# First layer's shift and scale: 128x128 weight blocks held and two columns moved, and six load buffers

## The chip, the cores and the metric

The kernel runs on one core of a Trainium2 chip. The core has a matrix engine (PE in the profile; its weight loads are listed apart as PEld), a vector engine (DVE), a scalar engine (ACT), a general engine (POOL), and a queue that issues transfers (SP). The metric is the device time of one execution in microseconds (us), lower being better. Three timed executions of the kernel before gave 2374.71, 2380.99 and 2374.34 us, so its median is 2374.71 us.

## The reference, cut to what matters

A two-layer backbone takes latent tokens x (1024 x 1024), context tokens ctx (256 x 1024) and two conditioning vectors. Each layer first turns the conditioning vectors into shifts, scales and gates, and the normalized tokens are modulated with them before any projection can run:

```
mod_lat = (silu_c @ mod_w[l] + mod_b[l])        # latent tokens
mod_ctx = silu_cc @ mod_w[l] + mod_b[l]         # context tokens
sh1, sc1, g1, sh2, sc2, g2 = split(mod_lat, 6)  # 1024 values each
h_lat = rms_norm(x, norm1_g[l]) * (1 + sc1) + sh1
h_ctx = rms_norm(ctx, norm1_g[l]) * (1 + csc1) + csh1
out   = mix(h_lat @ w_in, h_ctx @ w_in)         # retention and attention heads
```

Only sh1 and sc1 of the first layer matter here, each for both conditioning vectors: two vectors of 1024 times a 1024 x 2048 slice of `mod_w[0]`. The other ten parts are made later in another way.

## The kernel before, in words

Tokens lie transposed: a tile holds 128 channels (partitions) by up to 1024 tokens, so x is eight tiles `x_t[k]` and ctx one tile `ctx_t` of eight slices. A shift or a scale is therefore wanted as a column of 128 partitions per slice k: `sh1` and `gs1` (scale times gain), filled by `mod_cols`.

The start of the program does the following. SP issues the loads in the order in which the code names them, with at most eight in flight, and a load into a ring tile waits until the tile's last reader is done. ACT squares ctx and x, DVE adds the squares up (`start_sum`), PE sums over partitions (`norm_rstd`, tile nsum, a 128x128 block held and one column moved), POOL takes the power -0.5 (tile rs), and PE spreads the result over partitions (`norm_bc`, tile nbc). Beside that `mod_row(part, k)` loads a 128 x 1024 piece of `mod_w` (tile mw, a ring of three) and multiplies: the two conditioning columns `scc[:, k, :]` are held, 512 columns are moved, and the result is two rows of 1024 (tile modrow). Part 1 is the scale, part 0 the shift, eight pieces each. When a part's eight pieces are in, ACT copies the rows to SBUF (tile rsb), PE transposes them in eight steps into columns (tile mcol), and DVE adds the bias.

With the scale there, DVE multiplies all tokens by scale and norm (L266); with the shift there, ACT and DVE make the split operands h and hc (L276, L277), and the first projection begins: tiles pc (context) and pl (latent), by `mm3` (L75 to L77), three matmuls a product. Its weights (tile st, `in_wg`) are loaded and split by ACT (L80) and POOL (L81) beside the rest. All later work of the kernel follows from this projection.

A float32 matmul of the program stands in the trace as two passes, each with its own weight load. The instructions of one engine run in the order in which the tile framework leaves them, which for these lines is nearly that of the code.

Of the kernel before, what the change touches and what calls it, by code (L numbers as in the profile page):

```python
# [10 lines left out]
F32 = mybir.dt.float32  # L11
# [5 lines left out]
P = 128  # L17
D = 1024
KT = D // P
T = 1024  # L20
NTT = T // P
TC = 256
H = 512
# [3 lines left out]
NHID = 32  # L27
NW = 12
NPRO = 8
WCOL = 2 * H  # L30


def hybrid_retention_gqa_chunkmlp_kernel(tc, I, out):
    nc = tc.nc
    PSUM = bass.MemoryType.PSUM

    def open_pool(name, bufs=1, **kw):
        st = ExitStack()
        pool = st.enter_context(tc.tile_pool(name=name, bufs=bufs, **kw))
        return pool, st.close  # L40

    const, close_const = open_pool("const")
    stage, close_stage = open_pool("stage")
    sring = [stage.tile([P, WCOL], F32, name=f"st{i}") for i in range(3)]
    snext = [0]
    wpool, close_w = open_pool("wpool")
    wring = [wpool.tile([P, WCOL], F32R, name=f"wr{i}") for i in range(NW)]
    wnext = [0]
# [5 lines left out]
    def mm_tile(shape, name):  # L54
        if banks:
            return banks[0].tile(shape, F32, tag="b", bufs=8, name=name)
        return psum.tile(shape, F32, tag="mm", bufs=2, name=name)

    def aux_tile(shape, name):
        if banks:  # L60
            return banks[0].tile(shape, F32, tag="b", bufs=8, name=name)
        return psum.tile(shape, F32, tag="aux", bufs=4, name=name)
# [20 lines left out]
    def load_w(src, name, eng=nc.vector):  # L83
        st = st_tile()
        nc.sync.dma_start(st, src)
        hi, lo = w_tile(), w_tile()
        split(st, hi, lo, eng)
        return hi, lo


    ident = const.tile([P, P], F32, name="ident")
# [11 lines left out]
    scc = const.tile([P, KT, 2], F32, name="scc")  # L103
    nc.scalar.activation(scc, cc, AF.Silu)

    start, close_start = open_pool("start", side="right")
    startx, close_startx = open_pool("startx", side="right")
    ctx_t = start.tile([P, KT, TC], F32, name="ctx_t")
    x_t = [startx.tile([P, T], F32, tag="x0", bufs=8, name=f"x0_{k}") for k in range(KT)]
# [3 lines left out]
    gs1 = const.tile([P, 2, KT], F32, name="gs1")  # L113

    def mod_cols(part, dst):
        rsb = start.tile([2, D], F32, tag="rsb", bufs=1, name=f"rsb{part}")
        nc.scalar.copy(rsb, rows[part])
        mcol = aux_tile([P, 8, 2], f"mcol{part}")
        for j in range(8):
            nc.tensor.transpose(mcol[:, j, :], rsb[:, j * P:(j + 1) * P], ident[:2, :2])  # L120
        for s in range(2):
            nc.vector.tensor_tensor(dst[:, s, :], mcol[:, :, s], modb[:, 0, part * 8:part * 8 + 8], ALU.add)
            if part == 1:
                nc.vector.scalar_tensor_tensor(dst[:, s, :], dst[:, s, :], 1.0, gains[:, 0, :], ALU.add, ALU.mult)
# [66 lines left out]
    def norm_rstd(pool, ss, w):  # L191
        n = w // P
        pc = aux_tile([P, 8], "nsum")
        for t in range(n):
            nc.tensor.matmul(pc[:, t:t + 1], lhsT=ss[:, t * P:(t + 1) * P], rhs=ones, start=True, stop=True)
        ms = pool.tile([P, 8], F32, tag="ms", bufs=2, name="ms")
        nc.vector.tensor_scalar(ms[:, :n], pc[:, :n], 1.0 / D, EPS, ALU.mult, ALU.add)
        rs = pool.tile([P, 8], F32, tag="rs", bufs=2, name="rs")
        nc.gpsimd.tensor_tensor(rs[:, :n], ms[:, :n], mhalf[:, :n], ALU.pow)
        return rs  # L200

    def norm_bc(rs, w):
        pb = aux_tile([P, w], "nbc")
        for t in range(w // P):
            nc.tensor.matmul(pb[:, t * P:(t + 1) * P], lhsT=rs[:, t:t + 1].broadcast_to([P, P]), rhs=ident,
                             start=True, stop=True)
        return pb
# [4 lines left out]
    parts = [([ctx_t[:, k, :] for k in range(KT)], TC, 1,  # L212
              [(hc[k // 2][:, k % 2, 0, :], hc[k // 2][:, k % 2, 1, :]) for k in range(KT)])]
# [3 lines left out]
    def p_weight(gi, j):  # L217
        return load_w(I["wg"][gi, 2 * j:2 * j + 2].rearrange("k p n -> p k n"), f"g{gi}_{j}",
                      nc.vector if gi else nc.gpsimd)

    def start_sum(srcs, w, i):
        ss = start.tile([P, T], F32, tag="ssx", bufs=1, name=f"ssx{i}")[:, :w]
        for k in range(KT):
            sq = start.tile([P, T], F32, tag="sqx", bufs=2, name="sqx")[:, :w]
            nc.scalar.activation(sq, srcs[k], AF.Square)
            if k == 1:
                nc.vector.tensor_tensor(ss, sq0, sq, ALU.add)
            elif k > 1:
                nc.vector.tensor_tensor(ss, ss, sq, ALU.add)
            sq0 = sq  # L230
        return ss

    rows = [mm_tile([2, D], f"modrow{part}") for part in range(2)]

    def mod_row(part, k):
        st = start.tile([P, WCOL], F32, tag="mw", bufs=3, name=f"mw0_{k}_{part}")
        nc.sync.dma_start(st, I["mod_w"][0, k * P:(k + 1) * P, part * D:(part + 1) * D])
        for j in range(2):
            nc.tensor.matmul(rows[part][:, j * H:(j + 1) * H], lhsT=scc[:, k, :],
                             rhs=st[:, j * H:(j + 1) * H], start=(k == 0), stop=(k == KT - 1))  # L240

    W0 = []
    for i in range(4):
        mod_row(1, i)
        for k in (2 * i, 2 * i + 1):
            nc.sync.dma_start(x_t[k], I["xT"][k * P:(k + 1) * P, :])
    pbs = [norm_bc(norm_rstd(start, start_sum(parts[0][0], TC, 0), TC), TC)]
    for k in range(4, KT):
        mod_row(1, k)
        if k == 5:  # L250
            W0.append(p_weight(0, 0))
    ss_x = start_sum(x_t, T, 1)
    for k in range(KT):
        if k == 1:
            mod_cols(1, gs1)
        if k == 2:
            rs_x = norm_rstd(start, ss_x, T)
        if k == 3:
            for hf in range(2):
                pbs.append(norm_bc(rs_x[:, 4 * hf:4 * hf + 4], H))  # L260
        mod_row(0, k)
        if k in (0, 3, 5):
            W0.append(p_weight(0, len(W0)))
    for (srcs, w, s, _), pb in zip(parts, pbs):
        for k in range(KT):
            nc.vector.scalar_tensor_tensor(srcs[k], srcs[k], gs1[:, s, k:k + 1], pb, ALU.mult, ALU.mult)  # L266
    mod_cols(0, sh1)
    for i, (srcs, w, s, outs) in enumerate(parts):
        cw = w if i == 2 else TC
# [59 lines left out]
    for h in range(NH):  # L329
        for d in range(2):  # L330
            j = d * NH + h
# [235 lines left out]
    nt, close_nt = open_pool("nt")  # L567
    sring.append(nt.tile([P, WCOL], F32, name="st3"))
    yf_pool, close_yf = open_pool("yf")
# [273 lines left out]
    def up_first(l, F, s_d, e_d):  # L843

        for p0 in range(0, NPRO, 2):
            ps = [mm_tile([P, H], f"uf{l}_{p0 + d}") for d in range(2)]
# [81 lines left out]
    def layer_mlp(l, F, close_xt, s_d, e_d, x1_d, done):  # L928
# [5 lines left out]
        turns = iter(range(10000))  # L934
        mlp_up(l, F, s_d, lambda n: ring[next(turns) % 16], {p: e_d[p] for p in range(NPRO)})
        close_up()
# [7 lines left out]
    def scratch(l):  # L944
        s_d = [dram.tile([7, P, H], F32, name=f"s_d{l}_{p}") for p in range(16)]
        e_d = [dram.tile([P, H], F32, name=f"e_d{l}_{p}") for p in range(NPRO)]
        x1_d = dram.tile([KT, P, T], F32, name=f"x1_d{l}")
# [216 lines left out]
```

## Time and profile before

| what | value |
|---|---|
| timed executions, median | 2374.71 us |
| profiled execution, own time | 2382.32 us |
| its span, first to last instruction | 2380.5 us |
| PE busy | 2254.3 us, 95% of the span |
| DVE, ACT, POOL busy | 69%, 43%, 6% |
| chain that ended last, by engine | PE 78%, DVE 9%, DMA 6%, ACT 3% |
| mean granted clock of PE | 0.976 |

The page gives one execution's busy times, the chain of work that ended last followed back from the end, and the costliest groups of instructions. Times in the rows are microseconds from the start of the span; a mean duration is in nanoseconds. PE's clock has two levels in these rows, 2.4 GHz (1.00) and 1.2 GHz (0.50). A matmul's own duration contains the way through the array; what a stream of them costs is read from the starts, so from a row's duration divided by its count.

### The profile page before, as it was taken

The numbers are of one execution on the slowest core, as the hardware profiler recorded it, in microseconds if no ns is written. First come the engines' busy times: TensorE is split into PE (matmuls) and PEld (weight loads), VectorE is DVE, ScalarE is ACT, GpSimd is POOL, SyncE is SP. The second block draws the span as 40 slices with busy tenths as digits, with TensorE's granted clock in tenths as the row PEclk, the third lists the DMA queues.
The fourth block names the chain that finished last, engine by engine and source line by source line (L and its number), as shares of the span: only waits on it lengthen the run. The fifth ranks groups of instructions, "written<-read, shape, count | busy, mean of one in ns | idle before, by whom it ended". The sixth has DMA issues, their size and how long they took to land.

```text
span 2380.5 us, 28904 instructions
## 1 busy us (share of the span) xinstructions
PE 2254.3 (95%) x10412; PEld 1810.1 (76%) x10412; DVE 1651.0 (69%) x2750; ACT 1028.3 (43%) x1837; POOL 144.1 (6%) x133
## 2 busy tenths in 40 slices
PE   6998999989999999989999959999999999799999
PEld 1887787778887778867778847888878888677777
DVE  5656678699857776558888663444678755798885
ACT  3511112288745545554444333222465555544441
POOL 2322221100000000000000010000000000000000
PEclk9998999989999999999999979999999999899999
DMA  8244556430154664465454341114447444845442
GB/s 292 72 137 146 157 185 187 154 124 25 48 186 127 232 209 153 137 236 179 149 148 146 92 137 51 47 45 168 137 141 244 168 146 135 285 153 148 144 136 83
DMA packets 158688, 350.72 MB, mean 147 GB/s; under 512 B 16592, under 2 KB 30416, under 8 KB 158544
## 3 DMA queue, kind: packets, MB, share of 16 engines
q1 hardware_dynamic: 154960, 336.28, 43.6%
q0 software_dynamic: 3584, 12.58, 1.4%
q8 instruction: 82, 1.34, 0.2%
q14 instruction: 62, 0.51, 0.1%
HBM read 262.29 MB, written 86.51 MB: 147 GB/s over the span
## 4 chain that ended last, share of the span: by engine, by line
PE 78%; DVE 9%; DMA 6%; ACT 3%; issue 2%; POOL 1%; SPq 0%; DVEq 0%; ACTq 0%; POOLq 0%
PE dbd L75 5%; PE ub L75 4%; PE dbd L77 4%; PE dbd L76 4%; PE ub L76 4%; PE ub L77 4%; PE po L76 3%; PE po L77 3%; PE po L75 2%; PE ue L75 2%; PE ue L77 2%; PE ue L76 2%; PE ded L75 2%; PE ded L76 2%; PE ded L77 2%; PE pl L77 2%
## 5 line engine op out<-in xcount | busy, mean ns | idle before, releaser
L80 ACT CAST wr<-st 128x512 fp32r<-128x512 f32 (+4 forms) x422 | 281.0, 672 | 509.3 <-PE dbd L76 84.2
L81 DVE TENSOR_TENSOR wr<-st,wr 128x512 fp32r<-128x512 f32 (+4 forms) x418 | 310.3, 748 | 183.7 <-ACT wr L80 142.6
L75 PE MATMUL dbd<-sT,wr 128*128 128x512 f32 x384 | 157.1, 409 | 30.3 <-DVE xd L890 23.5
L75 PE MATMUL ub<-T,wr 128*128 128x512 f32 x384 | 153.1, 399 | 7.1 <-ACT wr L80 4.8
L75 PE MATMUL pl<-wr,h 128*128 128x512 f32 x384 | 154.8, 403 | 0.3 <-ACT zrl L484 0.3
L76 PE MATMUL dbd<-sT,wr 128*128 128x512 f32 x384 | 154.3, 402 | 0.0
L77 PE MATMUL dbd<-sT,wr 128*128 128x512 f32 x384 | 154.1, 401 | 0.0
L76 PE MATMUL pl<-wr,h 128*128 128x512 f32 x384 | 152.8, 398 | 0.0
L77 PE MATMUL pl<-wr,h 128*128 128x512 f32 x384 | 152.6, 397 | 0.0
L76 PE MATMUL ub<-T,wr 128*128 128x512 f32 x384 | 152.6, 397 | 0.0
L77 PE MATMUL ub<-T,wr 128*128 128x512 f32 x384 | 152.3, 397 | 0.0
L890 DVE SCALAR_TENSOR_TENSOR xd<-dbd,mcol,xd 128x512 f32<-128x512 f32 x152 | 113.1, 748 | 46.9 <-PE dbd L77 46.7
L75 PEld LDWEIGHTS dbd<-sT,wr 128*128 128x128 f32 x384 | 73.5, 191 | 58.2 <-DVE xd L890 29.8
L80 ACT CAST sT<-sT 128x512 fp32r<-128x512 f32 x128 | 78.7, 620 | 74.6 <-DMA sT<-s_d 71.8
L139 DVE SCALAR_TENSOR_TENSOR macc<-st,scc,macc 128x1024 f32<-128x1024 f32 x70 | 92.8, 1325 | 23.6 <-DMA st<-in_mod_w 23.0
L81 DVE TENSOR_TENSOR sT<-sT 128x512 fp32r<-128x512 f32 x128 | 87.4, 686 | 20.4 <-ACT sT L80 20.3
L75 PEld LDWEIGHTS ub<-T,wr 128*128 128x128 f32 x384 | 72.4, 189 | 26.9 <-ACT wr L80 6.1
L81 DVE TENSOR_TENSOR sB<-sB 128x512 fp32r<-128x512 f32 x96 | 66.0, 688 | 31.6 <-ACT sB L80 31.4
L77 PEld LDWEIGHTS dbd<-sT,wr 128*128 128x128 f32 x384 | 73.7, 192 | 18.2 <-DVE wr L81 0.2
L77 PEld LDWEIGHTS ub<-T,wr 128*128 128x128 f32 x384 | 72.7, 189 | 18.0
L76 PEld LDWEIGHTS dbd<-sT,wr 128*128 128x128 f32 x384 | 73.8, 192 | 16.2
L76 PEld LDWEIGHTS ub<-T,wr 128*128 128x128 f32 x384 | 72.6, 189 | 17.5
(363 smaller groups left out, 5844.1 us busy)
## 6 DMA issues: line engine op xcount, KB each, us to landing
st<-in_w SPq DMA_DIRECT2D x132, 512.0 KB, 4.4
s_d<-ur SPq DMA_DIRECT2D x208, 256.0 KB, 2.2
st<-in_mod_w SPq DMA_DIRECT2D x80, 512.0 KB, 4.4
sT<-s_d SPq DMA_DIRECT2D x128, 256.0 KB, 2.9
sB<-s_d SPq DMA_DIRECT2D x96, 256.0 KB, 3.1
st<-in_wo SPq DMA_DIRECT2D x32, 512.0 KB, 3.6
st<-in_wg SPq DMA_DIRECT2D x24, 512.0 KB, 4.7
mw<-in_mod_w SPq DMA_DIRECT2D x16, 512.0 KB, 5.7
```

Of the source, the lines that this page charges most:

```text
L75: nc.tensor.matmul(ps, lhsT=a_hi, rhs=b_hi, start=first, stop=False, skip_group_check=more)
L76: nc.tensor.matmul(ps, lhsT=a_hi, rhs=b_lo, start=False, stop=False, skip_group_check=more)
L77: nc.tensor.matmul(ps, lhsT=a_lo, rhs=b_hi, start=False, stop=last, skip_group_check=more)
L80: nc.scalar.copy(hi, src)
L81: eng.tensor_tensor(lo, src, hi.bitcast(F32), ALU.subtract)
L139: nc.vector.scalar_tensor_tensor(acc, st, scc[:, k, 0:1], acc, ALU.mult, ALU.add)
L890: nc.vector.scalar_tensor_tensor(o, ps_, g, o, ALU.mult, ALU.add)
```

## The change

The product is turned around. The two conditioning columns, which were held while 512 columns of `mod_w` moved, are now moved, and each 128x128 block of `mod_w` is held. A piece of 128 x 1024 is eight blocks, so a piece is eight float32 matmuls of two columns in place of two of 512. The results are columns at once, all eight of a part in one PSUM bank; the copy rsb and the 16 transposes go. The ring of three mw tiles becomes six fixed tiles. The loads are issued in another order: x and the pieces of the scale alternate, then the pieces of the shift with the weights of the first projection between them; the matmuls of a piece stand six loads behind its load.

```diff
--- before.py
+++ after.py
@@ -27,6 +27,7 @@
 NHID = 32
 NW = 12
 NPRO = 8
+NMW = 6
 WCOL = 2 * H
 
 
@@ -113,11 +114,7 @@
     gs1 = const.tile([P, 2, KT], F32, name="gs1")
 
     def mod_cols(part, dst):
-        rsb = start.tile([2, D], F32, tag="rsb", bufs=1, name=f"rsb{part}")
-        nc.scalar.copy(rsb, rows[part])
-        mcol = aux_tile([P, 8, 2], f"mcol{part}")
-        for j in range(8):
-            nc.tensor.transpose(mcol[:, j, :], rsb[:, j * P:(j + 1) * P], ident[:2, :2])
+        mcol = mcols[part]
         for s in range(2):
             nc.vector.tensor_tensor(dst[:, s, :], mcol[:, :, s], modb[:, 0, part * 8:part * 8 + 8], ALU.add)
             if part == 1:
@@ -230,37 +227,41 @@
             sq0 = sq
         return ss
 
-    rows = [mm_tile([2, D], f"modrow{part}") for part in range(2)]
-
-    def mod_row(part, k):
-        st = start.tile([P, WCOL], F32, tag="mw", bufs=3, name=f"mw0_{k}_{part}")
-        nc.sync.dma_start(st, I["mod_w"][0, k * P:(k + 1) * P, part * D:(part + 1) * D])
-        for j in range(2):
-            nc.tensor.matmul(rows[part][:, j * H:(j + 1) * H], lhsT=scc[:, k, :],
-                             rhs=st[:, j * H:(j + 1) * H], start=(k == 0), stop=(k == KT - 1))
+    mcols = [mm_tile([P, 8, 2], f"mcol{part}") for part in range(2)]
+    mws = [start.tile([P, WCOL], F32, name=f"mw{i}") for i in range(NMW)]
+    seq = [(part, k) for part in (1, 0) for k in range(KT)]
+
+    def mod_load(i):
+        part, k = seq[i]
+        nc.sync.dma_start(mws[i % NMW], I["mod_w"][0, k * P:(k + 1) * P, part * D:(part + 1) * D])
+
+    def mod_mm(i):
+
+        part, k = seq[i]
+        for j in range(8):
+            nc.tensor.matmul(mcols[part][:, j, :], lhsT=mws[i % NMW][:, j * P:(j + 1) * P], rhs=scc[:, k, :],
+                             start=(k + j == 0), stop=(k == KT - 1), skip_group_check=True)
 
     W0 = []
-    for i in range(4):
-        mod_row(1, i)
-        for k in (2 * i, 2 * i + 1):
-            nc.sync.dma_start(x_t[k], I["xT"][k * P:(k + 1) * P, :])
-    pbs = [norm_bc(norm_rstd(start, start_sum(parts[0][0], TC, 0), TC), TC)]
-    for k in range(4, KT):
-        mod_row(1, k)
-        if k == 5:
-            W0.append(p_weight(0, 0))
-    ss_x = start_sum(x_t, T, 1)
-    for k in range(KT):
-        if k == 1:
+    for i in range(2 * KT):
+        if i >= NMW:
+            mod_mm(i - NMW)
+        if i < KT:
+            nc.sync.dma_start(x_t[i], I["xT"][i * P:(i + 1) * P, :])
+        mod_load(i)
+        if i == 4:
+            pbs = [norm_bc(norm_rstd(start, start_sum(parts[0][0], TC, 0), TC), TC)]
+        if i in (8, 10, 12, 14):
+            W0.append(p_weight(0, len(W0)))
+        if i == 8:
+            ss_x = start_sum(x_t, T, 1)
+        if i == KT + NMW - 1:
             mod_cols(1, gs1)
-        if k == 2:
             rs_x = norm_rstd(start, ss_x, T)
-        if k == 3:
             for hf in range(2):
                 pbs.append(norm_bc(rs_x[:, 4 * hf:4 * hf + 4], H))
-        mod_row(0, k)
-        if k in (0, 3, 5):
-            W0.append(p_weight(0, len(W0)))
+    for i in range(2 * KT - NMW, 2 * KT):
+        mod_mm(i)
     for (srcs, w, s, _), pb in zip(parts, pbs):
         for k in range(KT):
             nc.vector.scalar_tensor_tensor(srcs[k], srcs[k], gs1[:, s, k:k + 1], pb, ALU.mult, ALU.mult)
```

On PE, at the start of the program, the order was this (modrow: the two rows; nsum and nbc: the norm; mcol: the transposed columns; pc: the first projection):

```order
L239 MATMUL modrow_143<-mw_0_1_144,scc 2x512 x2
L195 MATMUL nsum<-ones,ssx_168 128x1 x2
L205 MATMUL nbc<-ident,rs 128x128
L239 MATMUL modrow_143<-mw_1_1_150,scc 2x512 x2
L205 MATMUL nbc<-ident,rs 128x128
L239 MATMUL modrow_143<-mw_2_1_156,scc 2x512 x2
...
L239 MATMUL modrow_143<-mw_7_1_217,scc 2x512 x2
L239 MATMUL modrow_142<-mw_0_0_245,scc 2x512 x2
L120 MATMUL mcol_254<-ident,rsb_252 128x2 x8
L195 MATMUL nsum<-ones,ssx_221 128x1 x8
L239 MATMUL modrow_142<-mw_1_0_267,scc 2x512 x2
...
L239 MATMUL modrow_142<-mw_7_0_320,scc 2x512 x2
L120 MATMUL mcol_350<-ident,rsb_348 128x2 x8
L75 MATMUL pc_555<-wr_68,hc_122 128x256
```

And it is this in the changed kernel, where mcol is the product itself and mw the held blocks:

```order
L242 MATMUL mcol_143<-scc,mw_144 128x2 x8
L192 MATMUL nsum<-ones,ssx_160 128x1 x2
L202 MATMUL nbc<-ident,rs 128x128 x2
L242 MATMUL mcol_143<-scc,mw_145 128x2 x8
L242 MATMUL mcol_143<-scc,mw_146 128x2 x8
...
L242 MATMUL mcol_143<-scc,mw_145 128x2 x8
L192 MATMUL nsum<-ones,ssx_228 128x1 x8
L202 MATMUL nbc<-ident,rs 128x128 x8
L242 MATMUL mcol_142<-scc,mw_146 128x2 x8
...
L242 MATMUL mcol_142<-scc,mw_147 128x2 x8
L76 MATMUL pc_619<-wr_68,hc_122 128x256
```

The row of 128x2 is eight matmuls for one piece; sixteen such rows replace sixteen of two matmuls and two of eight transposes. All eight pieces of the shift now stand behind the sum and the spreading of x's norm; one stood ahead of the sum before, and two between.

On SP the loads of the same stretch were in this order (with the engines that a load waits for; DMAHW is the queue slot):

```order
L110 DMA ctx_t<-in_ctxT 128x8x256
L237 DMA mw_0_1_144<-in_mod_w 128x1024
L246 DMA x_0_108<-in_xT 128x1024
L246 DMA x_1_109<-in_xT 128x1024
L237 DMA mw_1_1_150<-in_mod_w 128x1024
...
L237 DMA mw_2_1_156<-in_mod_w 128x1024 [waits DMAHW2_49]
L246 DMA x_4_112<-in_xT 128x1024 [waits DMAHW3_49]
L246 DMA x_5_113<-in_xT 128x1024 [waits DMAHW4_49]
L237 DMA mw_3_1_162<-in_mod_w 128x1024 [waits DMAHW5_49,PE_49]
```

They are in this order now:

```order
L111 DMA ctx_t<-in_ctxT 128x8x256
L250 DMA x_0_108<-in_xT 128x1024
L236 DMA mw_144<-in_mod_w 128x1024
L250 DMA x_1_109<-in_xT 128x1024
L236 DMA mw_145<-in_mod_w 128x1024
...
L236 DMA mw_144<-in_mod_w 128x1024 [waits DMAHW1_49,PE_49]
L250 DMA x_7_115<-in_xT 128x1024 [waits DMAHW2_49]
L236 DMA mw_145<-in_mod_w 128x1024 [waits DMAHW3_49,PE_49]
...
L236 DMA mw_146<-in_mod_w 128x1024 [waits DMAHW5_49,PE_49]
L86 DMA st_62<-in_wg 128x2x512 [waits DMAHW6_49,Pool_49]
L236 DMA mw_147<-in_mod_w 128x1024 [waits DMAHW7_49,PE_49]
```

The first piece moved behind the first tile of x, and the first wait for PE moved from the fourth piece to the seventh. The projection's fourth weight load waits for POOL in both orders, and loads that wait for PE stand ahead of it.

On POOL the norm's power for x (rs, 128x8) stood between the second and third split of the projection's weights (wr):

```order
L199 TENSOR_TENSOR rs<-ms,mhalf 128x2
L81 TENSOR_TENSOR wr_69<-st_62,wr_68 128x1024
L81 TENSOR_TENSOR wr_71<-st_63,wr_70 128x1024
L199 TENSOR_TENSOR rs<-ms,mhalf 128x8
L81 TENSOR_TENSOR wr_73<-st_61,wr_72 128x1024
L81 TENSOR_TENSOR wr_75<-st_62,wr_74 128x1024
```

It stands ahead of all four now:

```order
L196 TENSOR_TENSOR rs<-ms,mhalf 128x2
L196 TENSOR_TENSOR rs<-ms,mhalf 128x8
L82 TENSOR_TENSOR wr_69<-st_62,wr_68 128x1024
L82 TENSOR_TENSOR wr_71<-st_63,wr_70 128x1024
L82 TENSOR_TENSOR wr_73<-st_61,wr_72 128x1024
L82 TENSOR_TENSOR wr_75<-st_62,wr_74 128x1024
```

The splits of the first two weights thus wait for the norm of x.

## Rows read from the trace of the kernel before

**Rows 1.** Windows of the start: length, busy of each engine, PE clock, DMA share, GB/s.

```profile
core 0: us, PE busy (x) PEld busy (x) DVE busy (x) ACT busy (x) POOL busy (x), PEclk, DMA share, GB/s
...
10.00:20.00 10.00, 8.95 (x18) 2.50 (x17) 6.66 (x11) 7.08 (x11) 0.71 (x1) 1.00 1.03 412
20.00:30.00 10.00, 8.03 (x15) 1.20 (x14) 4.58 (x4) 4.08 (x4) 1.32 (x1) 0.83 0.83 310
...
50.00:60.20 10.20, 5.32 (x19) 1.08 (x16) 7.35 (x12) 4.84 (x7) 2.36 (x1) 0.95 0.66 219
```

**Rows 2.** Chain that ended last, to 62 us: start, duration, what.

```profile
2.59 6.96 DMA mw<-in_mod_w
...
19.02 5.89 DMA mw<-in_mod_w
...
57.35 1.00 ACT rsb L117
...
60.26 0.58 PE pc L75
```

**Rows 3.** Groups of instructions on PE before the projection: busy, mean ns | idle before.

```profile
L239 PE MATMUL modrow<-mw,scc 128*2 128x512 f32 x64 | 33.8, 669 | 15.8 <-DMA mw<-in_mod_w 15.8
```

**Rows 4.** DMA issues, part 6 of the page: KB each, us to landing.

```profile
mw<-in_mod_w SPq DMA_DIRECT2D x16, 512.0 KB, 5.7
```

**Rows 5.** Timeline of PE: start, duration, operation, count [idle before].

```profile
9.68 3.57 PE L239 MATMUL modrow<-mw,scc 128*2 128x512 f32 x4 [9.68 <-DMA mw<-in_mod_w]
13.18 1.01 PE L195 MATMUL nsum<-ones,ssx 128*128 128x1 f32 x4
15.25 0.79 PE L205 MATMUL nbc<-ident,rs 128*128 128x128 f32 x2 [1.05 <-POOL rs L199]
15.97 3.01 PE L239 MATMUL modrow<-mw,scc 128*2 128x512 f32 x4
...
19.33 3.65 PE L239 MATMUL modrow<-mw,scc 128*2 128x512 f32 x8
...
37.80 1.95 PE L195 MATMUL nsum<-ones,ssx 128*128 128x1 f32 x16
39.68 3.59 PE L239 MATMUL modrow<-mw,scc 128*2 128x512 f32 x8
43.20 2.05 PE L205 MATMUL nbc<-ident,rs 128*128 128x128 f32 x16
```

**Rows 6.** Timeline of PE, the second of the four nsum passes at 13.18.

```profile
13.42 0.35 PE L195 MATMUL nsum<-ones,ssx 128*128 128x1 f32 x1
```

**Rows 7.** Timeline of PE, the last two of them.

```profile
13.63 0.57 PE L195 MATMUL nsum<-ones,ssx 128*128 128x1 f32 x2
```

**Rows 8.** Windows of 1 us where the clock changes, columns as in rows 1.

```profile
25.00:26.00 1.00, 1.00 (x2) 0.16 (x3) 1.00 (x1) 0.00 (x0) 0.00 (x0) 0.56 1.04 391
...
29.00:30.00 1.00, 1.00 (x3) 0.17 (x2) 0.00 (x0) 0.00 (x0) 1.00 (x1) 1.00 0.70 111
...
59.00:60.00 1.00, 0.06 (x1) 0.00 (x0) 0.90 (x3) 1.00 (x3) 0.00 (x0) 0.62 0.19 25
...
66.00:67.00 1.00, 1.00 (x10) 1.00 (x10) 0.69 (x2) 1.00 (x4) 0.31 (x1) 0.96 0.00 0
```

**Rows 9.** Timeline of PE, 55 to 60.9 us.

```profile
58.40 0.65 PE L120 MATMUL mcol<-ident,rsb 2*128 2x2 f32 x8 [1.43 <-ACT rsb L117]
```

**Rows 10.** Timeline of DVE, 37 to 60.5 us.

```profile
40.26 0.15 DVE L197 TENSOR_SCALAR ms<-nsum 128x8 f32<-128x8 f32 x1
```

**Rows 11.** Timeline of POOL, 13 to 47 us.

```profile
40.49 1.65 POOL L199 TENSOR_TENSOR rs<-ms,mhalf 128x8 f32<-128x8 f32 x1 [0.18 <-DVE gs L124]
43.65 2.35 POOL L81 TENSOR_TENSOR wr<-st,wr 128x1024 fp32r<-128x1024 f32 x1 [1.52 <-ACT wr L80]
```

## The prediction

> **What bounds the kernel now.** I read the windows of the start first: the change touches nothing behind the first projection except a few neighbours. The transfers run at 412 GB/s from 10 to 20 us and at 219 GB/s from 50 on [rows 1], so by then they are no longer the limit. The chain that ended last shows what is: it alternates between transfers of `mod_w` pieces and PE's matmuls of them, ends in the copy rsb at 57.35, and reaches the projection (pc) at 60.26 us [rows 2]. PE multiplies for 33.8 us there and waits 15.8 us for pieces [rows 3]: the ring of three lets a piece start only when an earlier one is used, and it lands 5.7 us after its issue [rows 4]. Behind 60 us PE is the bound, 95% busy on the page. The instruction order from there on is the same but for some splits, copies and head products near 60 to 130 us, so I take it that the time of the kernel moves by as much as the start of pc moves.
>
> **The price of the new product.** It replaces 64 passes of 512 columns by 256 passes (16 pieces, eight blocks, two passes each) that load a 128x128 block and move two columns. The trace has one kind of pass of nearly that form, the sum nsum, which holds 128x128 float32 and moves one column. It has two prices. At 37.80, 16 passes lead to the next matmul at 39.68 [rows 5]: 1.88/16 = 0.1175 us. At 13.18 the second pass starts at 13.42 [rows 6], and the last two start at 13.63 and at 13.63 + 0.57 - 0.35 = 13.85 [rows 7]: (13.85 - 13.42)/2 = 0.215 us. The reason is the clock. From 9.68 four passes of 512 columns took 3.57 us, from 19.33 eight took 3.65 [rows 5], so the first stretch ran at 1.2 GHz and the second at 2.4 GHz. (The clock column says 1.00 in both; it knows no level from before the first change. Later it shows 0.56 falling, then 1.00 again [rows 8].) So the load of a block costs twice as much at the low level, and the term hangs on the level: 256 x 0.215 = 55.0 us or 256 x 0.1175 = 30.1 us.
>
> Which level? PE starts low. It rose between 15.97 and 19.33 in a stretch of full-width moving [rows 5], fell near 25 after a pause of some 2 us, rose by 29 after the next full stretch, and fell within 59 to 60, when PE had done little but eight small transposes since 57 [rows 8, 9]. Each of its rises in the start came with PE moving columns without a pause. The changed kernel gives it hardly any: in a pass of 0.215 us two columns are moved against 512 in 0.9 us before, and only the two nbc groups move 128. No row shows a long stretch of block loads with almost no columns, so both prices stay possible; I take 0.215 because the new stream begins where nsum cost that much, after a pause and with no full-width work ahead of it.
>
> By the Trainium skill, "TensorE: Matmul & The Clock Gate", section "LDWEIGHTS (loading the stationary operand)", a weight load takes its number of columns over 1.2 GHz, about 0.107 us here, and the formula has no clock level in it. An estimate by it is 256 x 0.107 = 27.3 us. The rows at 13.42 and 13.63 disagree [rows 6, 7]: twice that at the low level. The same page, "Part 1: The HAM clock gate", says that low is the default and that activity of PE releases it; that agrees with the rise after 15.97 [rows 5], but whether loading blocks is activity it doesn't say, and no row here decides it.
>
> **The sum at the low level**, to the start of pc:
> - The first piece now stands behind x's first tile. Its data landed at 2.59 + 6.96 = 9.55 [rows 2]; one more 0.524 MB at 412 GB/s [rows 1, 4] is 1.27 us, plus 0.13 to the first matmul: 10.95.
> - 256 passes: 55.0. The ring is no limit. While x and pieces alternate a piece takes 2 x 1.27 = 2.5 us to come, PE uses 16 x 0.215 = 3.4 us for it, so loads run up to six ahead and the 15.8 us of waiting go: PE itself is late next.
> - nsum, 20 passes: 4.3. nbc, 20 passes: 2.05/16 = 0.13 at the high level [rows 5], doubled 0.25, so 5.0.
> - Two waits for the norm, which stand on PE's path because all later pieces are queued behind nbc. The first is 15.25 - 13.18 - 4 x 0.215 = 1.2 [rows 5]. The second, for x, was covered by shift pieces placed between; now it is bare: the way through the array 0.35 [rows 6], DVE's ms 0.15 [rows 10], POOL's power 1.65 [rows 11], together 2.2.
> - From the last product to pc, DVE's bias and ACT's first h and hc: 58.40 + 0.65 = 59.05 to 60.26 [rows 2, 9] is 1.2, with the end of the last pass 1.3.
>
> 10.95 + 55.0 + 4.3 + 5.0 + 1.2 + 2.2 + 1.3 = 80.0 us against 60.26, so +19.7 us. The copies rsb (1.00 us each [rows 2]) and 16 transposes are gone in this sum. The profiled execution of before took 2382.3 us, 7.6 us above the median shown, so it would be 2402.0 on that basis and **2394 us** on the median's.
>
> At no cost: POOL's four weight splits of 2.35 us [rows 11] now queue behind the power at about 47, end near 57 and are hidden by the eight shift pieces of 27 us; DVE's scaling of all tokens likewise. The fourth weight's load waits on SP for POOL, and the last piece behind it, but PE wants that one only at 75. Without the cover of the shift pieces these splits would end close to the projection, as in the first rival. After pc starts, PE ran at 1.2 GHz until about 66 before, and would again [rows 8]: no difference.
>
> Bounds of the price of a pass: the first gap of nsum, 13.42 - 13.18 = 0.24 us, gives 61.4 us and pc at 86, +26. The cheapest small pass, a transpose at 0.65/8 = 0.08 [rows 9] with two partitions in place of 128, gives 20.5 us; then the transfers end the wait: 15.7 MB (ctx 1, x 4, `mod_w` 8, weights 2 MiB) at 412 GB/s is 38 us from about 4, the last pieces' norm and tail make it about 47, -13.
>
> **The rivals.**
> (1) The loads count as work and the clock rises early. The first piece and its norm cost the low price, until about 17.5; pieces then follow their transfers, the eighth landing at 10.9 + 7 x 2.54 = 28.7 and used by 30.6; nsum 1.9, wait 2.1, nbc 2.0, eight pieces of 1.88 make 51.6, tail 1.3: pc at 52.9, -7.4. PE would also enter pc at 2.4 GHz and not lose up to half of the 5.8 us to 66; since ACT is filling the operands then, I give it 1. Result: -8.5, 2366 us, faster. For it: the high price at 37.80 and PE that would be busy without a pause; against it: no rise in the start without full-width moving. It decides where the clock rises before the fourth piece or so.
> (2) The second nbc group, 16 passes of full 128 columns, raises the clock and it stays up: eight pieces save 128 x (0.215 - 0.1175) = 12.5, leaving +7.2, 2382 us. Against it: what follows is the same thin stream.
> (3) The change works as meant but is hidden: pc is then held by weights or POOL's splits. In the fast case these end near 47, so they hold nothing unless the norm is late; a price within the spread of (1).
>
> **How the numbers follow.** Low level throughout 0.60, its own range 2389 to 2400 (passes at 0.20 to 0.24 us); rival 1 0.29, between 2362 (bound of the cheapest pass) and 2370; rival 2 0.11, 2377 to 2387. This kernel's measurement tells a change of about 0.3%, 7.1 us. Faster by more is below 2367.6, some three quarters of rival 1: 0.22. Slower by more is above 2381.8: the first case and a little of rival 2: 0.63. The rest, 0.15, is the same. The range reaches from 2364 to 2400; it leaves out a few hundredths at either end.
>
> **What would show it.** Right: nsum-like passes of the product 0.21 to 0.22 us apart, a granted clock of 0.50 (or no change to 1.00 with that spacing) up to the projection, PE without waits for mw, and pc near 80 us. Wrong: spacing near 0.12, PE waiting for pieces again, and pc near 53. If pc is near 80 and the total moves by less, some later stage had slack, which I priced at nothing. If pc is early and the total does not fall, the stage of the first projection was held by ACT.

## The result, and the profile after

The changed kernel took 2400.42 us (median of four executions, 2394.45 to 2401.43) beside 2377.55 for the kernel before (2374.34 to 2380.99): a ratio of 1.0091 (of all the executions, not of the two medians), 95% interval 1.0066 to 1.0116, or +21.6 us with 15.7 to 27.6. It is slower; 2394 had been predicted from a sum of +19.7 us, within 2364 to 2400. The median lies 0.4 us past the upper end; the number predicted stood on a median of 2374.71 for the kernel before, which is 2377.55 here. The profiled execution took 2400.83 us with a span of 2399.1, 18.6 more than the span of before. Timed again beside other executions of the kernel before it gave 2395.92, a ratio of 1.0065 [1.0042, 1.0088].

PE's timeline of the changed kernel up to the projection, which answers to [rows 5] (start, duration, line, operation, count [idle before]):

```profile
10.44 3.54 PE L242 MATMUL mcol<-scc,mw 128*128 128x2 f32 x16 [10.44 <-ACT sqx L222]
13.84 0.99 PE L192 MATMUL nsum<-ones,ssx 128*128 128x1 f32 x4
16.79 1.22 PE L202 MATMUL nbc<-ident,rs 128*128 128x128 f32 x4 [1.96 <-POOL rs L196]
17.80 23.89 PE L242 MATMUL mcol<-scc,mw 128*128 128x2 f32 x112
41.55 3.55 PE L192 MATMUL nsum<-ones,ssx 128*128 128x1 f32 x16
47.09 3.79 PE L202 MATMUL nbc<-ident,rs 128*128 128x128 f32 x16 [1.98 <-POOL rs L196]
50.66 24.19 PE L242 MATMUL mcol<-scc,mw 128*128 128x2 f32 x128
76.05 0.58 PE L76 MATMUL pc<-wr,hc 128*128 128x256 f32 x1 [1.20 <-ACT hc L277]
```

The second stretch of the product holds 112 passes in 41.55 - 17.80 = 23.75 us: 0.212 us a pass, close to the dear price of the two that the prediction read from nsum (0.215 [rows 6, 7]). The projection begins at 76.05, 15.8 us later than before [rows 2].

The product in that stretch as a group (busy, mean ns | idle before), against [rows 3]:

```profile
L242 PE MATMUL mcol<-scc,mw 128*128 128x2 f32 x256 | 51.6, 339 | 10.4 <-ACT sqx L222 10.4
```

Of the 15.8 us in [rows 3], 9.7 were the one wait ahead of the first piece (total, number, longest):

```profile
PE modrow L239 <- DMA mw<-in_mod_w: 15.8, 7, 9.7
```

That wait is still there, 10.44 us now. The page puts its end down to a square on ACT; the first piece itself was issued at 3.2 and took at least 7.1 us to land, which is as late. The other six waits, 6.1 us, are gone. The product is busy for 51.6 us, where it was 33.8. The chain that ended last no longer holds a transfer of `mod_w`; between the waits for POOL it is PE alone (start, duration, what):

```profile
18.00 23.68 PE mcol L242 x112
...
45.39 1.65 POOL rs L196
...
50.87 24.00 PE mcol L242 x128
74.89 0.18 DVE sh L119
...
76.05 0.58 PE pc L76
```

Windows of 10 us (length, then busy time and count of PE, PEld, DVE, ACT, POOL; clock; DMA share; GB/s), which answer to [rows 1]:

```profile
20.00:30.00 10.00, 10.00 (x48) 10.00 (x49) 4.90 (x4) 3.58 (x4) 0.00 (x0) 1.00 1.03 406
...
50.00:60.00 10.00, 10.00 (x65) 10.00 (x63) 9.82 (x15) 1.04 (x1) 5.19 (x3) 0.71 0.60 200
60.00:70.00 10.00, 10.00 (x48) 10.00 (x49) 0.00 (x0) 0.00 (x0) 1.15 (x1) 0.50 0.34 117
```

PE and its weight loads are busy without a gap, and that says nothing on the level. The count does: 48 passes in 10 us at a recorded 0.50, and 48 also from 20 to 30 us, where the column says 1.00 only because no change had been recorded yet. (A count takes in every pass that touches the window, so it is above the number of starts: at 0.212 us a pass 4.7 begin in a microsecond, and 6 or 7 are counted.) One stretch has more. In windows of 1 us, and as a row of the timeline from 51 to 54 us:

```profile
53.00:54.00 1.00, 1.00 (x12) 1.00 (x11) 1.00 (x3) 0.00 (x0) 0.99 (x1) 1.00 0.33 66
54.00:55.00 1.00, 1.00 (x8) 1.00 (x7) 1.00 (x2) 0.00 (x0) 0.00 (x0) 0.59 1.02 270
55.00:56.00 1.00, 1.00 (x7) 1.00 (x6) 1.00 (x3) 0.00 (x0) 0.00 (x0) 0.50 0.88 338
```

```profile
50.86 3.38 PE L242 MATMUL mcol<-scc,mw 128*128 128x2 f32 x29
```

After nbc's 16 passes of 128 moved columns the clock rose to 2.4 GHz: 12 passes counted in 1 us, and 3.38/29 = 0.117 us a pass at most. At 54.2, in the middle of the thin stream (the passes that move two columns), it fell to 1.2 GHz (7 passes counted from 55 on) although neither PE nor PEld had paused.

### The profile page after: what moved, and what is told of

The parts are those of the page before. It is cut to its first block, busy times and chain, and to the rows that moved or that the text cites. A ratio compares the mean times of both kernels' runs of the same rounds, so it can differ in the third digit from the quotient of the medians.

```text
span 2399.1 us, 29256 instructions
## 1 busy us (share of the span) xinstructions
PE 2272.5 (95%) x10588; PEld 1859.7 (78%) x10588; DVE 1649.5 (69%) x2750; ACT 1026.4 (43%) x1835; POOL 144.1 (6%) x133
## 4 chain that ended last, share of the span: by engine, by line
PE 76%; DVE 10%; DMA 7%; ACT 3%; issue 2%; POOL 1%; SPq 0%; DVEq 0%; ACTq 0%; POOLq 0%
PE ub L76 4%; PE ub L77 4%; PE ub L78 4%; PE dbd L76 4%; PE dbd L78 4%; PE dbd L77 4%; PE po L77 2%; PE po L76 2%; PE po L78 2%; PE ue L77 2%; PE ue L78 2%; PE ue L76 2%; PE mcol L242 2%; DMA sT<-s_d 2%; PE pl L78 2%
## 5 line engine op out<-in xcount | busy, mean ns | idle before, releaser
L76 PEld LDWEIGHTS dbd<-sT,wr 128*128 128x128 f32 x384 | 73.5, 191 | 63.9 <-DVE xd L891 32.5
L82 DVE TENSOR_TENSOR sB<-sB 128x512 fp32r<-128x512 f32 x96 | 66.0, 687 | 33.9 <-ACT sB L81 33.8
L77 PEld LDWEIGHTS ub<-T,wr 128*128 128x128 f32 x384 | 72.5, 189 | 17.3
```

Of the source, the lines that this page charges most:

```text
L76: nc.tensor.matmul(ps, lhsT=a_hi, rhs=b_hi, start=first, stop=False, skip_group_check=more)
L77: nc.tensor.matmul(ps, lhsT=a_hi, rhs=b_lo, start=False, stop=False, skip_group_check=more)
L82: eng.tensor_tensor(lo, src, hi.bitcast(F32), ALU.subtract)
```

## The experiments

Four accounts were set against each other. **A**: the loss is PE's level. A stream of blocks held with two columns moved neither raises the clock nor keeps it up, so each pass costs 0.212 in place of some 0.1175 us. **B**: turning the product around, or the new order of loads, is dear by itself, whatever the level. **C**: besides the late projection something lasting slows later stages. **D**: once up, the clock would stay up in the thin stream; it only lacks a start. The start of pc shows the stage alone, in one profiled execution each; the ratio the whole kernel.

**Repeat, nothing edited.**

> The changed kernel as it is, beside the next two, since its first ratio came from four executions of each kernel: its projection started 15.8 us later than before, which is 0.66%. Theory A (the loss is the late projection and nothing else lasting): the ratio comes out between 1.005 and 1.008, as it did in the run with 64 columns whose projection started 16.8 us later. Rival C (the changed start also costs some 3 us or more in later stages): 1.009 or more again.

2395.92 us, ratio 1.0065 [1.0042, 1.0088]; pc at 79.33. This time the second nbc did not raise the clock, and the last 128 passes took 27.31 us where they had taken 24.19. The projection was 19.1 us late and the end of the span 13.3; in the first profile these were 15.8 and 18.6. Later stages thus add or give back several microseconds from execution to execution. The ratio lies where A put it and under the 1.009 that C asked for. The intervals of the two ratios overlap, so nothing lasting is shown (C), and a few microseconds of it can't be excluded.

**128 columns moved.** The two columns are repeated 64 times; 126 of the 128 results are read by nobody.

```diff
-    mcols = [mm_tile([P, 8, 2], f"mcol{part}") for part in range(2)]
+    mcols = [mm_tile([P, 8, 128], f"mcol{part}") for part in range(2)]
...
-            nc.tensor.matmul(mcols[part][:, j, :], lhsT=mws[i % NMW][:, j * P:(j + 1) * P], rhs=scc[:, k, :],
-                             start=(k + j == 0), stop=(k == KT - 1), skip_group_check=True)
+            nc.tensor.matmul(mcols[part][:, j, :].rearrange("p (r s) -> p r s", s=2),
+                             lhsT=mws[i % NMW][:, j * P:(j + 1) * P],
+                             rhs=scc[:, k, :].unsqueeze(1).broadcast_to([P, 64, 2]),
+                             start=(k == 0 and j % 4 == 0), stop=(k == KT - 1), skip_group_check=True)
```

> The two columns are moved 64 times over in each pass (128 columns moved, 126 of the results not used), everything else as in the changed kernel. Theory A (the loss is PE's clock: holding blocks and moving two columns leaves PE at 1.2 GHz): with 128 columns moved the clock rises to 2.4 GHz within the first pieces and stays, a pass costs 0.12 to 0.13 us in place of 0.21, the projection starts near 54 us in place of 76, and the time is about 20 us under the changed kernel, 0.2 to 0.5% under the kernel before. Rival B (a load of a 128x128 float32 block costs 0.21 us in this stream whatever the clock, or the order of the shift pieces behind the norm makes the loss): passes stay at 0.21 us or more, the projection starts at 76 us or later, the time is that of the changed kernel or worse.

2371.18 us, ratio 0.9961 [0.9943, 0.9979]: faster than before. Its timeline of PE and its group of the product:

```profile
16.03 15.82 PE L242 MATMUL mcol<-scc,mw 128*128 128x128 f32 x122
...
37.40 13.79 PE L242 MATMUL mcol<-scc,mw 128*128 128x128 f32 x122
52.06 0.39 PE L76 MATMUL pc<-wr,hc 128*128 128x256 f32 x1 [0.87 <-ACT hc L279]
```

```profile
L242 PE MATMUL mcol<-scc,mw 128*128 128x128 f32 x256 | 32.5, 289 | 10.8 <-ACT sqx L222 10.8
```

The same 256 loads of the same blocks, with 64 times the columns moved, take 32.5 us in place of 51.6. The last 122 passes cost 13.79/122 = 0.113 us each. The rise shows in the counts of its windows:

```profile
19.00:20.00 1.00, 1.00 (x7) 1.00 (x6) 0.61 (x1) 0.14 (x1) 0.00 (x0) 1.00 1.03 410
20.00:21.00 1.00, 1.00 (x10) 1.00 (x9) 0.05 (x1) 0.91 (x1) 0.00 (x0) 1.00 1.02 406
21.00:22.00 1.00, 1.00 (x12) 1.00 (x11) 1.00 (x1) 0.00 (x0) 0.00 (x0) 1.00 1.02 406
```

From 7 passes counted in a microsecond to 12 within 2 us; the low spacing ends at 20.3. This is what A says and what B excludes: neither the turn nor the order is dear at 2.4 GHz. With the padding nsum also stands elsewhere on PE (behind 4 passes of the first piece, where it was behind 16). That is not the cause: in the next run it stands behind 8, and the clock stays low.

**64 columns moved.** As above with 64 in place of 128 (62 of them unread).

> As the run with 128 columns, with 64 columns moved in each pass. [...] The projection starts between 62 and 77 us. Rival B: 76 us or later, nothing depends on the columns.

2393.2 us, ratio 1.0053 [1.0033, 1.0073]; pc at 77.04. Here PE stayed low up to the projection:

```profile
49.29 26.55 PE L242 MATMUL mcol<-scc,mw 128*128 128x64 f32 x124
```

```profile
60.00:70.00 10.00, 10.00 (x49) 10.00 (x49) 0.00 (x0) 0.00 (x0) 0.50 (x1) 1.00 0.32 106
```

26.55/124 = 0.214 us a pass, with 49 counted in 10 us, about as in the thin stream: 62 more columns changed neither the price nor the level. (No change had been recorded, so the clock column says 1.00.) The start of pc lies at the edge of what was expected under A (62 to 77) and within what B gave (76 or later), so this run alone does not tell the two apart; the run with 128 columns does.

**Old product, new order and six tiles.**

```diff
-        for j in range(8):
-            nc.tensor.matmul(mcols[part][:, j, :], lhsT=mws[i % NMW][:, j * P:(j + 1) * P], rhs=scc[:, k, :],
+        for j in range(2):
+            nc.tensor.matmul(rows[part][:, j * H:(j + 1) * H], lhsT=scc[:, k, :],
+                             rhs=mws[i % NMW][:, j * H:(j + 1) * H], start=(k == 0), stop=(k == KT - 1))
```

(and in `mod_cols` the copy rsb and the transposes of before).

> The old product (two columns held, 512 moved, rows copied and transposed) with the changed kernel's six buffers and order of loads and pieces. Theory A: PE is at 2.4 GHz from about 18 us as in the kernel before, the waits of 15.8 us for pieces shrink to a few us, the projection starts near 50 to 54 us, and the time is 0.2 to 0.5% under the kernel before. Rival B in the form that order or buffers make the loss: the projection starts near 70 us or later.

2371.63 us, ratio 0.9973 [0.9958, 0.9987]; pc at 55.01. The order and the tiles alone are a gain. The waits for pieces behind the first, 6.1 us before, are 0.7 now; the wait ahead of the first piece stays (10.5):

```profile
L246 PE MATMUL modrow<-mw,scc 128*2 128x512 f32 x64 | 31.8, 647 | 11.2 <-ACT sqx L226 10.5 <-DMA mw<-in_mod_w 0.7
```

pc came 5.2 us earlier, a little less than the expected 50 to 54, which took all 15.8 us for waits that could shrink. Some of the gain went to the clock. It fell at 35.1, before the pause for x's norm began at 35.5 and behind 24 thin passes (eight transposes of two columns, 16 of nsum), so nbc went at the low price (16 passes in 3.78), and part of the product behind it:

```profile
32.45 1.95 PE L196 MATMUL nsum<-ones,ssx 128*128 128x1 f32 x16
34.33 1.19 PE L246 MATMUL modrow<-mw,scc 128*2 128x512 f32 x2
36.51 3.78 PE L206 MATMUL nbc<-ident,rs 128*128 128x128 f32 x16 [0.98 <-POOL rs L200]
```

What made it fall here, and not behind the same nsum with 128 columns moved, is not settled.

**New product, old order, ring of three.**

```diff
+    def mod_row(part, k):
+        st = start.tile([P, WCOL], F32, tag="mw", bufs=3, name=f"mw0_{k}_{part}")
...
-            nc.tensor.matmul(mcols[part][:, j, :], lhsT=mws[i % NMW][:, j * P:(j + 1) * P], rhs=scc[:, k, :],
+            nc.tensor.matmul(mcols[part][:, j, :], lhsT=st[:, j * P:(j + 1) * P], rhs=scc[:, k, :],
```

> The new product (blocks held, two columns moved) in the order of the kernel before, with its ring of three buffers. Theory A: the passes cost 0.21 us through almost the whole start, 55 us in all, so the projection starts at 76 to 82 us and the time is 0.6 to 1.0% over the kernel before. Rival B in the form that the order makes the loss: near 60 us, no difference to the kernel before.

2392.64 us, ratio 1.0054 [1.0035, 1.0073]; pc at 74.11, 13.9 us late with the loads ordered as before (76 to 82 was expected). The product alone makes the loss:

```profile
9.35 3.55 PE L235 MATMUL mcol<-scc,mw 128*128 128x2 f32 x16 [9.35 <-DMA mw<-in_mod_w]
...
41.88 31.03 PE L235 MATMUL mcol<-scc,mw 128*128 128x2 f32 x160
74.11 0.58 PE L75 MATMUL pc<-wr,hc 128*128 128x256 f32 x1 [1.20 <-ACT hc L272]
```

Behind nbc the clock rose here too and fell again at 45.9, so the last 160 passes took 31.03 us and not the 34 that 0.213 each would make.

The two parts do not add. -5.2 and +13.9 would make +8.7, and both together made +15.8 and +19.1: the slow product fills the waits for pieces even with three tiles, so the new order has nothing left to win. Its later first piece (10.44 for 9.35) and longer first wait for the norm (1.96 for 1.05) make the 1.9 us to the first profile; in the repeat, where the clock did not rise behind nbc, another 3.1 come from that.

**A burst ahead.** Six float32 matmuls of 512 columns on the identity, whose result nobody reads, stand ahead of the first piece: in the kernel with 128 columns, and in the changed kernel; then twelve in the changed kernel.

```diff
+    wm = aux_tile([P, 4, P], "warm")
+    for j in range(6):
+        nc.tensor.matmul(wm, lhsT=ident, rhs=ident.unsqueeze(1).broadcast_to([P, 4, P]), start=True, stop=True)
```

> 128 columns moved in each pass, and six float32 matmuls of 512 columns on the identity ahead of the first piece, whose result nobody reads, while PE has nothing to do. Theory A: the clock is at 2.4 GHz when the first piece lands, the scale's pieces then follow their transfers, and the projection starts 0.5 to 2 us earlier than in the run without it (52.1 us): 0.3 to 0.5% under the kernel before. Rival: the first pieces were bound by transfers anyway and the projection starts at 52 us.

> The changed kernel with the same six matmuls ahead of its first piece. Theory A (two moved columns don't hold the clock): the first piece or two run at 0.12 us a pass, then the clock falls and the rest costs 0.21 us again; the projection starts between 72 and 76 us. Rival D (two columns can't raise the clock but hold it once it is up): passes stay at 0.12 us, the projection starts near 53 us.

> The changed kernel with twelve float32 matmuls of 512 columns on the identity ahead of its first piece (24 passes, nobody reads the result), so that they end when the norm's first sum and the first piece begin, without the pause of 4.3 us that the run with six left. Theory A (two moved columns don't hold the clock): the clock is at 2.4 GHz when the first pieces begin, their passes cost 0.12 us, and it falls within some pieces though PE is never idle; the rest costs 0.21 us. Rival D (two columns can't raise the clock but hold it while PE doesn't pause): passes stay at 0.12 us up to the wait for x's norm.

With 128 columns: 2371.21 us, ratio 0.9962 [0.9948, 0.9976], no better than without the burst, and pc at 54.94, later than 52.06; a miss. The clock rose at 7.4, fell at 14.2 after a pause of 2.91 us ahead of nsum, rose again at 17.6, fell once more at 34.7, in the second wait for the norm, where it had stayed up without the burst, and rose at 41.5. That wait is the same 1.21 us in both, so why it fell in one alone is not settled. In the changed kernel with six matmuls (one execution, 2397.72; pc at 79.31) the clock rose at 4.6 and fell in the pause of 4.30 us ahead of nsum, before the thin stream began: nothing follows for D. Twelve matmuls (one execution, 2394.15) leave no pause; the burst runs to 14.57, and the thin stream begins at 14.94:

```profile
1.35 13.38 PE L247 MATMUL warm<-ident 128*128 128x512 f32 x24 [1.35 <-POOL ident masks.py:199]
14.57 0.50 PE L192 MATMUL nsum<-ones,ssx 128*128 128x1 f32 x4
14.94 10.38 PE L242 MATMUL mcol<-scc,mw 128*128 128x2 f32 x58
```

```profile
15.00:16.00 1.00, 1.00 (x11) 1.00 (x10) 0.89 (x2) 0.00 (x0) 0.65 (x1) 1.00 1.00 401
16.00:17.00 1.00, 1.00 (x11) 1.00 (x10) 0.40 (x1) 0.56 (x1) 0.98 (x1) 1.00 1.04 418
17.00:18.00 1.00, 1.00 (x8) 1.00 (x7) 0.47 (x1) 1.00 (x2) 0.00 (x0) 0.65 1.03 414
```

It begins at 2.4 GHz and falls to 1.2 at 17.3, with PE and PEld full in every window. D falls: the thin stream does not hold the clock, whether nbc (above, to 54.2) or a burst stands ahead of it. pc came at 78.57, near the 79.33 of the repeat.

**128 columns, and the norm's wait covered.** The spreading of x's norm is put after two pieces of the shift.

```diff
+        if i == KT + NMW + 1:
             for hf in range(2):
                 pbs.append(norm_bc(rs_x[:, 4 * hf:4 * hf + 4], H))
```

> 128 columns moved in each pass, and the spreading of x's norm two pieces later in the code, so that pieces of the shift stand between sum and spreading on PE. Theory A: the bare wait of about 1.2 us for the norm goes, PE has no pause in which its clock could fall, the projection starts at 50 to 51.5 us (52.1 without the move), 0.4 to 0.5% under the kernel before. Rival: with the weights' splits on POOL behind the norm, the projection starts at 52 us as without it.

2370.89 us beside 2379.71, ratio 0.9963 [0.9949, 0.9976]. The stage is the shortest of all:

```profile
31.66 1.84 PE L192 MATMUL nsum<-ones,ssx 128*128 128x1 f32 x16
33.37 2.03 PE L242 MATMUL mcol<-scc,mw 128*128 128x128 f32 x16
35.49 1.38 PE L202 MATMUL nbc<-ident,rs 128*128 128x128 f32 x10
...
50.92 0.39 PE L76 MATMUL pc<-wr,hc 128*128 128x256 f32 x1 [0.87 <-ACT hc L280]
```

No idle time stands ahead of this second nbc, and the clock stayed at 2.4 GHz from 17.8 us on, through the start of the projection. Without the cover it had fallen at 54.4, behind the start of pc; the gaps between the projection's first products are the same in both (0.48 and 0.38 us), so this difference is seen but not explained. The window with the projection's start in it, where the version without the cover has 0.83:

```profile
50.00:60.00 10.00, 8.16 (x56) 7.25 (x56) 8.58 (x18) 9.64 (x26) 3.06 (x4) 1.00 0.29 77
```

It beats both kernels (-8.8 us, and pc 9.3 us earlier than in [rows 2]); against the version with 128 columns alone the total shows no difference that can be measured.

## Why the prediction was right

The first profile's terms, from PE's timeline, beside the predicted ones (us):

| term | predicted | measured | repeat |
|---|---|---|---|
| start of the first piece | 10.95 | 10.44 | 10.58 |
| 256 passes | 55.0 | 3.40 + 23.75 + 24.19 = 51.3 | 54.5 |
| nsum | 4.3 | 4.5 | 4.5 |
| nbc | 5.0 | 4.6 | 4.6 |
| waits for the norm | 1.2 + 2.2 | 1.96 + 1.98 | 1.96 + 1.99 |
| last product to pc | 1.3 | 1.2 | 1.2 |
| pc starts | 80.0 | 76.05 | 79.33 |

- **The price of a pass** was the step on which all hung, and the low level was the right choice: 0.212 us against 0.215. The reason given, that this stream moves hardly any columns, is what the padded versions tested: same loads, other level, 0.113. That no full-width work stood ahead of it, the other part of the reason, was not what mattered: behind the burst of twelve the stream fell all the same. The Trainium skill, "TensorE: Matmul & The Clock Gate", section "LDWEIGHTS (loading the stationary operand)", prices a load by its columns over 1.2 GHz and has no clock level in the formula; an estimate by it is 128/1.2, some 0.107 us. The trace is near that at 2.4 GHz (0.113 a pass) and not at 1.2 GHz (0.212).
- **The wait for pieces** was misread, at no cost to the sum. The 15.8 us hold the 9.7 ahead of the first piece, which stayed (10.44) and which the sum itself keeps, as 10.95; only 6.1 could go. They went, and PE itself was late next, as the product of 51.6 us busy with no idle time for mw shows.
- **Rival 1** (loads count as work) was the one with a real chance against the forecast. Its time for the stage, pc at 52.9, is what 128 columns gave, 52.06; with two columns the clock did not rise, and where it was up it fell. So its condition was false. Its sum came out with some luck: the scale was used up at 31.7 for 30.6, and the second wait was 1.2 for 2.1.
- **Rival 2** (the second nbc raises the clock and it stays) happened by half: raised in one profile of two, from 50.8 to 54.2, and it did not stay. The 3.1 us that this saved (24.19 for 27.31) are the largest miss of the sum.
- **Rival 3** (hidden by the weights or POOL) had nothing to act on: POOL's last split ended at 61.2 (57 was predicted; it waited for ACT), 14.9 us ahead of pc:

```profile
58.80 2.35 POOL L82 TENSOR_TENSOR wr<-st,wr 128x1024 fp32r<-128x1024 f32 x1 [4.81 <-ACT wr L81]
```

- **The first wait for the norm** was mis-sized: 1.96 for 1.2. POOL's power of two columns took 1.62 us, and 0.71 in the kernel before and with 64 and 128 columns moved. Why the same instruction has two durations was not tested:

```profile
15.11 1.62 POOL L196 TENSOR_TENSOR rs<-ms,mhalf 128x2 f32<-128x2 f32 x1 [13.81 <-DVE ms L194]
```

- **That the kernel moves by what pc moves** held only roughly, over two executions together: +15.8 at pc and +18.6 at the end in one, +19.1 and +13.3 in the other. That the total came closer to +19.7 than pc did in the first is luck. The predicted +19.7 lies within both measured intervals (15.7 to 27.6 and 10.0 to 20.9).

## What to carry to other kernels

A PE that is busy in every window can still run at half its clock, so read the spacing of the passes (a row's duration by its count) before you price a new form of matmul. A total of waits can hold the one at the start of the program, which six tiles and the new order left as it was here (9.7 and 10.4 us): look at the longest. Turning a product around so that the large operand is held makes it a stream of weight loads; here that stream was cheap at 2.4 GHz (0.117 us a pass at most) and neither reached nor held that level by itself, and repeating the moved columns 64 times, at no cost in time, made the stage 24 to 27 us shorter (52.06 for 76.05 and 79.33). Change the order of the loads and the form of the product apart: here one was a gain of 0.3% that the other hid entirely. Whether the turned product with 128 columns is any faster than the old one in the new order is not shown: the intervals of 0.9961 and 0.9973 overlap.

## What the runs showed of the hardware

- The level went with the moved columns, not with how full PE was: with 2 and 64 columns PE and PEld were busy 10.00 of 10 us and the clock stayed at or fell to 1.2 GHz; two columns ran at 2.4 GHz only in spells behind wider work (50.8 to 54.2 behind nbc, to 17.3 behind the burst). With 128 the clock rose to 2.4 GHz at 20.3 us and stayed through the product; with the burst ahead it fell once in between, at 34.7. No number of columns between 64 and 128 was run.
- A pass that loads a 128x128 float32 block costs the same with 2 and 64 columns moved at 1.2 GHz (0.212 and 0.214 us), and with 128 moved at 2.4 GHz no more (0.113) than with two (0.117 at most) or nsum's one (0.1175).
- In the kernel before the clock stayed at 2.4 GHz over 3.7 us of transposes of 128 columns: from 628.95 to 632.65 PE did nothing else, with pauses of 0.65 and 0.28 us between them, and the window inside shows 1.00:

```profile
629.00:632.00 3.00, 2.06 (x15) 1.35 (x14) 3.00 (x7) 2.69 (x6) 0.00 (x0) 1.00 0.26 49
```

- A burst of work ahead of the stage bought nothing here: six matmuls raised the clock at 4.6 us, and it fell in the pause of 4.30 us behind them.
- The Trainium skill, "TensorE: Matmul & The Clock Gate", section "HAM oscillation — how this bites in real kernels", advises for matmuls that are thin in M to restructure the loop or to pad M, where waits for transfers let the clock fall. What was padded here is the moved columns of each pass, and it helped (pc at 52.06 for 76.05) though PE waited for no transfer behind the first piece: the thin stream itself lost the level.
